# The last layer's MLP output projection as seven block products instead of eight

## The chip, the cores and the metric

The kernel runs on one core of a Trainium2 chip. The metric is the device time in microseconds of one execution. The kernel before has a median of 1990.09 us over three runs (1988.89 to 1991.19).

## What is computed

A decoder trunk of two layers for 512 tokens of width 1024, all in fp32. Each layer mixes tokens in three parallel branches and then runs an MLP; a final RMS norm follows. The part that matters here is the MLP of the second layer and the final norm:

```python
h2 = rms_norm(x, norm2_w[l]) * (1.0 + sc2) + sh2
x = x + g2 * (jnp.square(jax.nn.relu(h2 @ w_up[l])) @ w_down[l])   # 1024 -> 4096 -> 1024
...
return rms_norm(x, final_norm_w)
```

`g2` has one value for each of the 1024 channels.

## The kernel before

Activations are held transposed, with channels on the 128 partitions and the 512 tokens along the free axis (`xt[m]`, eight tiles). Every fp32 matmul is made of three fast ones: both operands are split into a high part H and a low part L, and `mm3` (L199 to L201) issues H·H, L·H and H·L into one PSUM bank. The weights are stationary and the activations move, 512 columns in each matmul.

A planner walks through `Job`s. A Job is two output blocks of 128 channels over eight blocks of 128 inputs; its weights come in two pieces of 128x1024 (four input blocks by 256 channels). `emit_split` fetches a piece by DMA into `raw`, ACT casts it to H (`wH`, L469), DVE subtracts to get L (`wL`, L470), and 24 matmuls use it. A tile framework gives every engine its own order of instructions from that plan, by dependences, priorities and buffers.

The MLP runs in four quarters of 1024 hidden channels. In each, four up Jobs (192 matmuls) end in relu and square on ACT (L1491, L1492) and a split into `uH` and `uL` on ACT and DVE (L192, L193); then four down Jobs (192 matmuls) end in one DVE instruction for each of the eight blocks, x += g2·y (L1504). In the last layer and last quarter, the last two down Jobs go in halves of 256 tokens (192 half-width matmuls in place of 96), so that the end can start on the first half; their weights and results have the names `paH`, `paL`, `po` and `qk`. There the updated x is transposed on PE (`to_tokens`, L1453) to get tokens on partitions, ACT sums squares (L1456), DVE multiplies by the norm's weight (L1458), and `final` scales by 1/rms (L1470 on ACT, L1472 on DVE) and writes out by DMA (L1473).

Of the kernel before, what the change touches and what calls it, by code (L numbers as in the profile page):

```python
# [106 lines left out]
def paired(fin, a, b):  # L107

    a.fin = b.fin = fin
    a.left = b.left = 2  # L110
    ps = a.pieces() + b.pieces()
    for p in ps:
        p.keep = True
    return [Unit(p, c) for c in HALVES for p in ps]

# [35 lines left out]
def tile_trunk(ctx: ExitStack, tc: tile.TileContext, io, out, depth=DEPTH):  # L151
# [15 lines left out]
    def tmp():  # L167
        return tf.tile([P, T], F32, name="tmp", tag="tmp")
# [278 lines left out]

    def emit_split(p):
        j = p.job
        w = sum(n for _, n in j.cols)  # L450
# [23 lines left out]
    def emit_mm(u, ks):  # L474
        p, c = u.p, u.c
        j = p.job
        if j.ps is None:
# [164 lines left out]
    def layer(l, lys):  # L642
# [790 lines left out]

        w_up = io["w_up"][l].rearrange("(k p) c -> p k c", p=P)
        w_dn = io["w_down"][l].rearrange("(k p) c -> p k c", p=P)
        if last:
            xw = [pa.tile([P, 4, P], F32, name="xw", tag="pa") for _ in range(8)]
            sqs = fixed(32).rearrange("p (a b) -> p a b", a=4)
            s4 = fixed(4)
            r4 = fixed(4)  # L1440
            q4 = fixed(4)
            fwb = [pa.tile([P, T], F32, name="fwb", tag="pa") for _ in range(2)]
            for i in range(2):
                sync.dma_start(fwb[i], io["final_norm_w"][i * T:(i + 1) * T].rearrange("(o d) -> o d", o=1).broadcast_to([P, T]))
        else:
            yield Stream(fin, "next", ada(l + 1, "next", [2, 3, 0, 1, 4, 5, 8, 9, 6, 7, 10, 11], pa, "pa", 2.0))
# [13 lines left out]

        def final(c):
            t = slice(c.start // P, c.stop // P)
            s_, r_, q_ = s4[:, t], r4[:, t], q4[:, t]
# [136 lines left out]
```

## Time and profile before

| | us |
|---|---|
| median of three runs (1988.89 to 1991.19) | 1990.09 |
| the profiled execution's own time | 1988.82 |
| its span (the trace) | 1987.1 |
| PE busy | 1949.8 (98%) |
| DVE busy | 1277.8 (64%) |
| ACT busy | 871.6 (44%) |

The MLP of the last layer starts at about 1626 us of the span; its last matmul starts at 1977.06. All tables below are of the same profiled execution. Times in them are microseconds from the start of the span unless marked ns; a PE instruction's printed duration overlaps the next one's, so the spacing of starts tells what a matmul costs.

### The profile page before, as it was taken

The page shows a single profiled execution, that of the slowest core. Times are in us where ns is not written, and L with a number is a line of the kernel's source. Part 1 is how long each engine was busy: PE and PEld are TensorE (multiplying, and loading weights), DVE is VectorE, ACT ScalarE, POOL GpSimd, SP SyncE. Part 2 cuts the span into 40 slices and gives each one's busy share as a digit, 9 for nine tenths or more (in the row PEclk, how much of TensorE's full clock was granted, in tenths as well). Part 3 has the DMA queues.
Part 4 walks back from the last instruction along what each step waited for, and adds up shares of the span by engine and source line. Part 5 has one row for each costly group of instructions (what it writes and reads, how often), then busy time and mean ns, then how long its engine had stood idle before and what let it go on. Part 6 is the DMA issues. An engine that isn't in the chain of part 4 may idle for free.

```text
span 1987.1 us, 26736 instructions
## 1 busy us (share of the span) xinstructions
PE 1949.8 (98%) x9940; PEld 1613.1 (81%) x9940; DVE 1277.8 (64%) x2368; ACT 871.6 (44%) x1562; POOL 94.9 (5%) x135
## 2 busy tenths in 40 slices
PE   7998999999999999999999999999999999999998
PEld 5787777788888988888897787778888898888887
DVE  4799768967846986333578985687575572333334
ACT  4453626733534534142545445384343354233243
POOL 0110210100000000000001101001000000000000
PEclk9999999999999999999999999999999999999999
DMA  9864353552444694333425433425233422333321
GB/s 288 222 168 131 107 153 108 156 188 87 136 127 142 223 371 161 95 103 98 118 86 139 113 103 90 118 70 151 67 104 108 156 95 96 96 96 96 95 96 43
DMA packets 249623, 258.30 MB, mean 130 GB/s; under 512 B 33828, under 2 KB 208212, under 8 KB 249492
## 3 DMA queue, kind: packets, MB, share of 16 engines
q1 hardware_dynamic: 248912, 256.45, 42.3%
q8 instruction: 78, 1.28, 0.3%
q14 instruction: 53, 0.43, 0.1%
q10 hardware_dynamic: 356, 0.14, 0.0%
q0 software_dynamic: 224, 0.00, 0.0%
HBM read 232.81 MB, written 6.42 MB: 120 GB/s over the span
## 4 chain that ended last, share of the span: by engine, by line
PE 89%; DVE 5%; DMA 2%; issue 1%; ACT 1%; POOL 1%; SPq 0%; ACTq 0%; POOLq 0%; DVEq 0%
PE acc L199 25%; PE acc L201 25%; PE acc L200 25%; PE qk L225 2%; PE po L1001 1%; PE tr L992 1%; DVE wL L470 1%; PE po L907 1%; PE tr L894 1%; DVE sc L823 1%; PE qk L1204 1%; DVE m L822 1%; DMA araw<-in_ada_w_dram 1%; PE po L201 1%; PE po L200 1%
## 5 line engine op out<-in xcount | busy, mean ns | idle before, releaser
L199 PE MATMUL acc<-aH,wH 128*128 128x512 f32 x1544 | 613.6, 398 | 10.6 <-DVE paL L193 5.3
L201 PE MATMUL acc<-aH,wL 128*128 128x512 f32 x1544 | 606.7, 393 | 0.9 <-DVE wL L470 0.8
L200 PE MATMUL acc<-aL,wH 128*128 128x512 f32 x1544 | 606.5, 393 | 0.0
L469 ACT CAST wH<-raw 128x1024 fp32r<-128x1024 f32 (+2 forms) x290 | 295.2, 1026 | 289.5 <-PE acc L200 250.5
L470 DVE TENSOR_TENSOR wL<-raw,wH 128x1024 fp32r<-128x1024 f32 (+2 forms) x290 | 343.3, 1199 | 16.0 <-ACT wH L469 8.3
L199 PEld LDWEIGHTS acc<-aH,wH 128*128 128x128 f32 x1544 | 291.4, 189 | 72.8 <-DVE paL L193 6.1
L201 PEld LDWEIGHTS acc<-aH,wL 128*128 128x128 f32 x1544 | 291.0, 188 | 62.5 <-DVE wL L470 2.1
L200 PEld LDWEIGHTS acc<-aL,wH 128*128 128x128 f32 x1544 | 291.6, 189 | 57.6 <-issue 0.7
L199 PE MATMUL acc<-uH,wH 128*128 128x512 f32 x448 | 174.9, 390 | 0.0
L201 PE MATMUL acc<-uH,wL 128*128 128x512 f32 x448 | 174.6, 390 | 0.0
L200 PE MATMUL acc<-uL,wH 128*128 128x512 f32 x448 | 174.3, 389 | 0.0
L193 DVE TENSOR_TENSOR uL<-tmp,uH 128x512 fp32r<-128x512 f32 x64 | 43.9, 691 | 189.2 <-ACT uH L192 189.2
L1491 ACT ACTIVATE tmp<-acc 128x512 f32<-128x512 f32 x60 | 35.3, 592 | 220.0 <-PE acc L201 220.0
L1504 DVE SCALAR_TENSOR_TENSOR x<-acc,slab,x 128x512 f32<-128x512 f32 (+1 forms) x64 | 43.8, 716 | 128.7 <-PE acc L201 128.7
L343 DVE SCALAR_TENSOR_TENSOR aacc<-araw,slab,aacc 128x512 f32<-128x512 f32 x140 | 104.0, 749 | 5.7 <-DMA araw<-in_ada_w_dram 4.1
L200 PEld LDWEIGHTS acc<-uL,wH 128*128 128x128 f32 x448 | 84.1, 188 | 17.4
L201 PEld LDWEIGHTS acc<-uH,wL 128*128 128x128 f32 x448 | 84.1, 188 | 17.4
L199 PEld LDWEIGHTS acc<-uH,wH 128*128 128x128 f32 x448 | 84.1, 188 | 17.1
L882 DVE TENSOR_TENSOR_SCAN tmp<-tmp 128x512 f32<-128x512 f32 (+1 forms) x64 | 52.5, 826 | 21.5 <-ACT tmp L875 21.4
L675 POOL TENSOR_TENSOR tmp<-tmp,slab 128x512 f32<-128x512 f32 (+1 forms) x20 | 31.6, 1581 | 719.5 <-DVE tmp L674 708.6
L1312 DVE SCALAR_TENSOR_TENSOR tmp<-tg,acc 128x512 f32<-128x512 f32 x16 | 11.0, 685 | 67.0 <-PE acc L201 67.0
L822 DVE MAX8 m<-sc 128x8 f32<-128x256 f32 (+2 forms) x96 | 52.8, 552 | 1.2 <-POOL sc L800 0.2
(307 smaller groups left out, 3022.1 us busy)
## 6 DMA issues: line engine op xcount, KB each, us to landing
araw<-in_ada_w_dram SPq DMA_DIRECT2D x192, 256.0 KB, 5.4
raw<-in_w_in_dram SPq DMA_DIRECT2D x96, 512.0 KB, 4.1
raw<-in_w_up_dram SPq DMA_DIRECT2D x64, 512.0 KB, 4.6
raw<-in_w_down_dram SPq DMA_DIRECT2D x64, 512.0 KB, 4.6
raw<-in_w_in_dram SPq DMA_DIRECT2D x56, 256.0 KB, 4.4
acb<-acd SPq DMA_DIRECT2D x32, 256.0 KB, 4.6
raw<-in_w_br_ssd_dram SPq DMA_DIRECT2D x16, 512.0 KB, 4.5
raw<-in_w_out_dram SPq DMA_DIRECT2D x16, 512.0 KB, 4.2
```

The lines of the kernel that those rows point to most:

```text
L193: dve.tensor_sub(L, src, H)
L199: pe.matmul(ps, a[0], b[0], start=start, stop=False)
L200: pe.matmul(ps, a[0], b[1], start=False, stop=False)
L201: pe.matmul(ps, a[1], b[0], start=False, stop=stop)
L225: pe.matmul(ps, q[hh][:, cq], k[n][hh][:, ck], start=n == 0, stop=n == 1)
L343: dve.scalar_tensor_tensor(a, raw, cs[:, k:k + 1], a, op0=ALU.mult, op1=ALU.add)
L469: act.copy(H[:, :w], src)
L470: dve.tensor_sub(L[:, :w], src, H[:, :w])
L822: dve.max(out=m8, in_=sc[tb])
L882: dve.tensor_tensor_scan(out=nv, data0=nv, data1=nv, initial=1.0, op0=ALU.mult, op1=ALU.bypass)
L1491: act.activation(r, ps, AF.Relu)
L1504: dve.scalar_tensor_tensor(xt[m][:, c], ps[:, c], mod[l][:, M_G2 + m:M_G2 + m + 1], xt[m][:, c], op0=ALU.mult, op1=ALU.add)
```

## The change

The first layer keeps its code. In the second, `last_mlp` replaces the four quarters. The up Jobs stay. For the down projection of a quarter, the tokens are cut in two halves of 256, the hidden channels into even and odd blocks of 512, and the output channels into two halves of 512; the product of 2x2 by 2x2 blocks is made of seven block products in Winograd's form of Strassen's identity. Now the activations are stationary (blocks of 128x128 tokens) and the weights move, 512 columns in each matmul, so results have tokens on partitions. A product is 4 hidden blocks x 2 token blocks x 3 = 24 matmuls of 512 columns; a quarter has 168, in the order P1, P6, P2, P7, P5, P4, P3.

- Sums of activations (`us`, four of 128x256 for each pair of hidden blocks) and their splits (`ua`, `ub`, `uc`, `ud`) are made on DVE and ACT after the up Jobs.
- Weights of a quarter are fetched raw into eight tiles `rd`; sums of weights (`tt`, or in place in `rd`) are made by eight DVE instructions of 128x1024, and `split_form` makes 14 pieces of 128x1024, each used by 12 matmuls.
- Each product has two PSUM results (`dn`). In the first quarter ACT copies them into twelve accumulators `yacc` in SBUF, later DVE adds to these (`plus`), 16 additions in a quarter, since P1 goes to two accumulators.
- x is transposed to tokens during the first quarter (32 transposes) and put aside in DRAM (`xtd`), and fetched back (`xtok`) in the last quarter.
- In the last quarter the accumulators are combined (`last_of`), multiplied by g2 (`rowb`), added to x, squared on ACT, scaled and written out. The half-width matmuls are gone.

```diff
+class Prod(Job):
+    def __init__(self, name, form, lhs, banks, evac, need=(), pre=None):
+        super().__init__(name, None, 4, [], [0, 1], None, evac, need=need, dve=0.65, pre=pre, step=2)
+        self.form, self.lhs, self.banks = form, lhs, banks
...
+    def split_form(p):
+        j = p.job
+        src = j.form(p.k0 // 2)
+        H, L = (wp.tile([P, 1024], F32R, name=n, tag=n) for n in ("wH", "wL"))
+        with tc.high_priority():
+            act.copy(H, src)
+            dve.tensor_sub(L, src, H)
+        p.H, p.L = ([X[:, k * T:(k + 1) * T] for k in range(2)] for X in (H, L))
+    def product(u):
+        p = u.p
+        j = p.job
+        if j.ps is None:
+            if j.pre is not None:
+                j.pre()
+            j.ps = j.banks()
+        for i in range(2):
+            for k in range(p.nk):
+                kk = p.k0 + k
+                a = [X[:, i * P:(i + 1) * P] for X in j.lhs(kk)]
+                mm3(j.ps[i], a, (p.H[k], p.L[k]), kk == 0, kk == j.nk - 1)
+            if p.last:
+                with tc.high_priority():
+                    j.evac(i, j.ps[i])
+        p.left -= 1
+        if p.last:
+            j.left -= 1
+            j.fin.add(j.name)
...
+            def to_tokens(tb, i):
+                ps = tr_bank()
+                for m in range(4):
+                    pe.transpose(ps[:, m * P:(m + 1) * P], xt[4 * i + m][:, tb * P:(tb + 1) * P], ident)
+                t = tmp()
+                act.copy(t, ps)
+                sync.dma_start(xtd[:, 2 * tb + i, :], t)
...
+            def plus(key, i, src):
+                if (key, i) not in y:
+                    y[key, i] = tf.tile([P, T], F32, name="yacc", tag="yacc", bufs=12)
+                    act.copy(y[key, i], src)
+                else:
+                    dve.tensor_add(y[key, i], y[key, i], src)
+            def into_x(n, i, tb, d, src=None):
+                o = xf[tb, d] = y[n, i]
+                if src is None:
+                    dve.tensor_mul(o, o, rowb["g", d])
+                    dve.tensor_add(o, o, xtok[tb, d])
+                else:
+                    t = tmp()
+                    dve.tensor_mul(t, src, rowb["g", d])
+                    dve.tensor_add(o, o, t)
...
+            def final(tb, d):
+                t = slice(tb, tb + 1)
+                s_, r_, q_ = s4[:, t], r4[:, t], q4[:, t]
+                dve.tensor_add(s_, sqs[:, tb, 0:1], sqs[:, tb, 1:2])
+                rstd_cols(s_, r_, q_)
+                for i in (1 - d, d):
+                    o = xf[tb, i]
+                    if i == d:
+                        dve.scalar_tensor_tensor(o, o, r_, rowb["f", i], op0=ALU.mult, op1=ALU.mult)
+                    else:
+                        act.activation(o, o, AF.Identity, scale=r_)
+                    sync.dma_start(o2[tb * P:(tb + 1) * P, i * T:(i + 1) * T], o)
+            def early(tb, d):
+                squares(tb, d)
+                dve.tensor_mul(xf[tb, d], xf[tb, d], rowb["f", d])
+            def last_of(n, i, ps):
+                def add_(a, b):
+                    dve.tensor_add(y[a, i], y[a, i], y[b, i])
+                if n == 1:
+                    for tb in (i, 2 + i):
+                        back(tb)
+                elif n == 2:
+                    into_x(2, i, i, 0)
+                    early(i, 0)
+                elif n == 7:
+                    add_(7, 1)
+                    add_(4, 7)
+                    into_x(4, i, 2 + i, 0)
+                elif n == 5:
+                    add_(7, 5)
+                    into_x(7, i, 2 + i, 1)
+                    early(2 + i, 1)
+                    add_(3, 1)
+                    add_(3, 5)
+                    into_x(3, i, i, 1)
+                elif n == 4:
+                    into_x(4, i, 2 + i, 0, ps)
+                    squares(2 + i, 0)
+                    final(2 + i, 0)
+                elif n == 3:
+                    into_x(3, i, i, 1, ps)
+                    squares(i, 1)
...
+                        split(r1[:, 0:V], aH, aL)
+                        split(r2, bH, bL)
+                        dve.tensor_add(S[0], r1[:, V:], r2[:, V:])
+                        dve.tensor_sub(S[1], S[0], r1[:, 0:V])
+                        split(c_, cH, cL)
+                        dve.tensor_sub(S[2], r1[:, 0:V], r1[:, V:])
+                        dve.tensor_sub(S[3], r2[:, 0:V], S[1])
+                        split(d_, dH, dL)
...
+                def sums(h, R=R, F=F):
+                    F[3, h], F[2, h] = (wp.tile([P, 1024], F32, name="tt", tag="tt", bufs=4) for _ in range(2))
+                    dve.tensor_sub(F[3, h], R[1, 1, h], R[0, 1, h])
+                    dve.tensor_add(F[2, h], F[3, h], R[0, 0, h])
+                def t1(h, R=R):
+                    dve.tensor_sub(R[0, 1, h], R[0, 1, h], R[0, 0, h])
+                    return R[0, 1, h]
+                def t4(h, R=R, F=F):
+                    dve.tensor_sub(F[2, h], R[1, 0, h], F[2, h])
+                    return F[2, h]
...
+                prods = [(1, raw_(0, 0), "a11"), (6, f_(2), "s2"), (2, raw_(1, 0), "a12"), (7, f_(3), "s3"),
+                         (5, t1, "s1"), (4, t4, "a22"), (3, raw_(1, 1), "s4")]
+                yield from add([Prod(f"p{n}{qt}", form, lhs(a), banks, evac_of(n), pre=exp_ln_set if end and n == 1 else None)
+                                for n, form, a in prods])
...
-            xw = [pa.tile([P, 4, P], F32, name="xw", tag="pa") for _ in range(8)]
-            sqs = fixed(32).rearrange("p (a b) -> p a b", a=4)
-            s4 = fixed(4)
-            r4 = fixed(4)
-            q4 = fixed(4)
-            fwb = [pa.tile([P, T], F32, name="fwb", tag="pa") for _ in range(2)]
...
+            yield from last_mlp()
+            return
...
-        def to_tokens(m, c):
-            tbs = range(c.start // P, c.stop // P)
-            pt = tr_bank()
-            for tb in tbs:
-                pe.transpose(pt[:, tb * P:(tb + 1) * P], xt[m][:, tb * P:(tb + 1) * P], ident)
-            q = tmp()
-            for tb in tbs:
-                act.activation(q[:, tb * P:(tb + 1) * P], pt[:, tb * P:(tb + 1) * P], AF.Square,
-                               accum_out=sqs[:, tb, m:m + 1])
-                dve.tensor_mul(xw[2 * tb + m // 4][:, m % 4, :], pt[:, tb * P:(tb + 1) * P],
-                               fwb[m // 4][:, m % 4 * P:(m % 4 + 1) * P])
...
-                        if last:
-                            to_tokens(m, c)
-                            if m == NK - 1:
-                                final(c)
```

On DVE, before, in a down projection of the middle of the MLP. `wL` is the low part of a weight piece, and L1504 adds a result to x:

```order
L470 TENSOR_TENSOR wL<-raw,wH 128x1024 x2
L1504 SCALAR_TENSOR_TENSOR x<-acc,slab,x 128x512 x2
L470 TENSOR_TENSOR wL<-raw,wH 128x1024 x2
L1504 SCALAR_TENSOR_TENSOR x<-acc,slab,x 128x512 x2
L470 TENSOR_TENSOR wL<-raw,wH 128x1024 x2
```

On DVE, after, in the products of the third quarter (L463 makes a piece's low part, L1531 adds a result to its accumulator, L1639, L1640 and L1647 are sums of weights):

```order
L463 TENSOR_TENSOR wL<-rd,wH 128x1024
L1639 TENSOR_TENSOR tt<-rd 128x1024
L463 TENSOR_TENSOR wL<-tt,wH 128x1024
L1531 TENSOR_TENSOR yacc<-yacc,dn 128x512
L1640 TENSOR_TENSOR tt<-tt,rd 128x1024
L1531 TENSOR_TENSOR yacc<-yacc,dn 128x512
L463 TENSOR_TENSOR wL<-tt,wH 128x1024
L1639 TENSOR_TENSOR tt<-rd 128x1024
L463 TENSOR_TENSOR wL<-rd,wH 128x1024
```

Between two splits there stand now a sum of weights and additions to accumulators, where two x additions stood between pairs of splits.

On DVE, before, at the end of the last quarter, up to the first half's output:

```order
L1504 SCALAR_TENSOR_TENSOR x<-po,slab,x 128x256
L1504 SCALAR_TENSOR_TENSOR x<-qk,slab,x 128x256
L1458 TENSOR_TENSOR xw<-tr,fwb 128x128 x4
L1464 TENSOR_REDUCE slab<-slab 128x2
L362 TENSOR_SCALAR slab<-slab 128x2
```

On DVE, after, in the middle of the last quarter's products (L1563, L1568, L1537 and L1538 are steps of the output on accumulators; `udL` is the low part of the last pair's S3 and S4):

```order
L1563 TENSOR_TENSOR yacc<-yacc,rowb 128x512 x2
L1568 TENSOR_TENSOR yacc<-yacc 128x512 x2
L463 TENSOR_TENSOR wL<-tt,wH 128x1024
L1531 TENSOR_TENSOR yacc<-yacc,dn 128x512 x2
L1568 TENSOR_TENSOR yacc<-yacc 128x512 x2
L1537 TENSOR_TENSOR yacc<-yacc,rowb 128x512 x2
L1538 TENSOR_TENSOR yacc<-yacc,xtok 128x512 x2
L202 TENSOR_TENSOR udL<-us,udH 128x512
L1647 TENSOR_TENSOR tt<-rd,tt 128x1024
L1531 TENSOR_TENSOR yacc<-yacc,dn 128x512 x2
```

The output's steps stand among the pieces' splits instead of behind the last result, and eight of them stand ahead of `udL` and of the sum L1647 that the next products take.

On PE, after, the place that takes this `udL` (the matmuls on `ubH` and `ubL` are of another product):

```order
L208 MATMUL dn<-wH,ubH 128x512
L209 MATMUL dn<-wL,ubH 128x512
L210 MATMUL dn<-wH,ubL 128x512
L210 MATMUL dn<-wH,udL 128x512 x2
L208 MATMUL dn<-wH,ubH 128x512 x2
L208 MATMUL dn<-wH,udH 128x512 x2
L209 MATMUL dn<-wL,ubH 128x512
```

The last two matmuls of P7 stand behind work of P4, which the order took ahead of them.

Elsewhere in the program rows move by a few places (PE at some 50 rows, some DMA issues of the first layer's weights), and buffers lie at other addresses.

## Rows read from the trace of the kernel before

**Rows 1.** Page, parts 1 and 4: busy time of each engine; the last chain by engine.
```profile
PE 1949.8 (98%) x9940; PEld 1613.1 (81%) x9940; DVE 1277.8 (64%) x2368; ACT 871.6 (44%) x1562; POOL 94.9 (5%) x135
...
PE 89%; DVE 5%; DMA 2%; issue 1%; ACT 1%; POOL 1%; SPq 0%; ACTq 0%; POOLq 0%; DVEq 0%
```

**Rows 2.** Windows of the last layer's MLP; the columns stand in the first line.
```profile
core 0: us, PE busy (x) PEld busy (x) DVE busy (x) ACT busy (x) POOL busy (x), PEclk, DMA share, GB/s
1717.00:1804.00 87.00, 87.00 (x386) 72.03 (x385) 29.42 (x32) 28.88 (x40) 0.00 (x0) 1.00 0.31 97
1804.00:1891.00 87.00, 87.00 (x386) 72.03 (x385) 29.41 (x32) 28.88 (x40) 0.00 (x0) 1.00 0.31 97
1891.00:1977.00 86.00, 86.00 (x484) 75.34 (x483) 34.39 (x70) 37.03 (x101) 0.00 (x0) 1.00 0.18 61
1977.00:1988.00 11.00, 1.17 (x7) 0.54 (x6) 3.81 (x14) 3.18 (x12) 0.00 (x0) 0.72 0.26 95
```

**Rows 3.** Groups by line, 1629 to 1988 us: names, shapes, count | busy, mean ns | idle before.
```profile
L470 DVE TENSOR_TENSOR wL<-raw,wH 128x1024 fp32r<-128x1024 f32 x54 | 63.6, 1217 | 0.0
...
L193 DVE TENSOR_TENSOR uL<-tmp,uH 128x512 fp32r<-128x512 f32 x32 | 22.0, 692 | 120.5 <-ACT uH L192 120.5
...
L1504 DVE SCALAR_TENSOR_TENSOR x<-acc,slab,x 128x512 f32<-128x512 f32 x28 | 20.1, 750 | 86.2 <-PE acc L201 86.2
...
L1453 PE MATMUL tr<-slab,x 128*128 128x128 f32 x32 | 5.7, 282 | 0.2 <-DVE x L1504 0.2
```

**Rows 4.** PE in order of time, down projection: start, us, line, operation.
```profile
1720.27 0.39 PE L199 MATMUL acc<-aH,wH 128*128 128x512 f32 x1
1720.50 0.39 PE L200 MATMUL acc<-aL,wH 128*128 128x512 f32 x1
1720.72 0.39 PE L201 MATMUL acc<-aH,wL 128*128 128x512 f32 x1
1720.95 0.39 PE L199 MATMUL acc<-aH,wH 128*128 128x512 f32 x1
```

**Rows 5.** Chain of waits near the end: start, us, engine, tile, line (half-width matmuls).
```profile
1974.11 0.12 PE qk L199
1974.22 0.12 PE qk L200
1974.35 0.12 PE qk L201
```

**Rows 6.** DVE in order of time, back to back: start, us, line, operation.
```profile
641.55 0.42 DVE L410 TENSOR_TENSOR tmp<-tmp 128x256 f32<-128x256 f32 x1
641.89 0.69 DVE L470 TENSOR_TENSOR paL<-raw,paH 128x512 fp32r<-128x512 f32 x1
642.49 0.42 DVE L410 TENSOR_TENSOR tmp<-tmp 128x256 f32<-128x256 f32 x1
...
667.29 4.85 DVE L343 SCALAR_TENSOR_TENSOR aacc<-araw,slab,aacc 128x512 f32<-128x512 f32 x7
...
1078.97 1.19 DVE L470 TENSOR_TENSOR wL<-raw,wH 128x1024 fp32r<-128x1024 f32 x1
1080.10 0.73 DVE L798 SCALAR_TENSOR_TENSOR sc<-tmp,slab,sc 128x512 f32<-128x512 f32 x1
```

**Rows 7.** All engines in order of time, the last ten microseconds.
```profile
1977.06 0.28 PE L201 MATMUL qk<-uH,paL 128*128 128x256 f32 x1
...
1980.63 0.16 DVE L365 TENSOR_TENSOR slab<-slab 128x2 f32<-128x2 f32 x1 [0.51 <-ACT slab L364]
1980.82 0.16 DVE L366 TENSOR_TENSOR slab<-slab 128x2 f32<-128x2 f32 x1
...
1981.42 1.33 ACT L1470 ACTIVATE xw<-xw,slab 128x512 f32<-128x512 f32 x2 [0.82 <-DVE slab L368]
1981.42 0.88 DVE L1472 TENSOR_SCALAR xw<-xw,slab 128x512 f32<-128x512 f32 x2
1981.93 1.79 SPq L1473 DMA_DIRECT2D out_dram<-xw  x4
```

**Rows 8.** Page, part 6: DMA issues, count, size of each, median us to landing.
```profile
raw<-in_w_down_dram SPq DMA_DIRECT2D x64, 512.0 KB, 4.6
```

**Rows 9.** Windows of other stages, columns as in rows 2.
```profile
150.00:200.00 50.00, 44.66 (x201) 35.47 (x200) 49.28 (x109) 17.90 (x29) 1.50 (x5) 0.93 0.44 129
```

More of the change, by code (lines that the diff above doesn't have):

```diff
@@ L446, in add @@
                                      op0=ALU.add, op1=ALU.subtract)
+    def split_form(p):
[25 more added lines that the diff above has]
+            j.fin.add(j.name)
     def emit_split(p):
         j = p.job
+        if isinstance(j, Prod):
+            split_form(p)
+            return
         w = sum(n for _, n in j.cols)
@@ L476, in emit_mm @@
         j = p.job
+        if isinstance(j, Prod):
+            product(u)
+            return
         if j.ps is None:
@@ L1436, in layer @@
         if last:
-            xw = [pa.tile([P, 4, P], F32, name="xw", tag="pa") for _ in range(8)]
-            sqs = fixed(32).rearrange("p (a b) -> p a b", a=4)
-            s4 = fixed(4)
-            r4 = fixed(4)
-            q4 = fixed(4)
-            fwb = [pa.tile([P, T], F32, name="fwb", tag="pa") for _ in range(2)]
[L1443 to L1446, printed above, removed]
@@ L1461, in final @@
-        def final(c):
-            t = slice(c.start // P, c.stop // P)
-            s_, r_, q_ = s4[:, t], r4[:, t], q4[:, t]
-            dve.tensor_reduce(out=s_, in_=sqs[:, t, :], op=ALU.add, axis=mybir.AxisListType.X)
-            rstd_cols(s_, r_, q_)
-            for tb in range(t.start, t.stop):
-                for i in range(2):
-                    o = xw[2 * tb + i]
-                    if i:
-                        act.activation(o, o, AF.Identity, scale=r4[:, tb:tb + 1])
-                    else:
-                        dve.tensor_scalar(o, o, r4[:, tb:tb + 1], None, op0=ALU.mult)
-                    sync.dma_start(o2[tb * P:(tb + 1) * P, i * T:(i + 1) * T], o.rearrange("p m c -> p (m c)"))
+            yield from last_mlp()
@@ L1475, in dn_pre @@
+            return
+        yield Stream(fin, "next", ada(l + 1, "next", [2, 3, 0, 1, 4, 5, 8, 9, 6, 7, 10, 11], pa, "pa", 2.0))
+        ss = SumSq()
         def dn_pre():
             exp_ln_set()
-            if not last:
-                lys[l + 1] = begin(l + 1)
-                scale_of(l + 1, lys[l + 1]["A1"], M_SC1, "norm1_w")
+            lys[l + 1] = begin(l + 1)
+            scale_of(l + 1, lys[l + 1]["A1"], M_SC1, "norm1_w")
         for qt in range(4):
@@ L1506, in evac_dn @@
                     if qt == 3:
-                        if last:
-                            to_tokens(m, c)
-                            if m == NK - 1:
-                                final(c)
-                        else:
-                            ss.add(xt[m], c, m)
-                            if m == NK - 1:
-                                norm1(l + 1, lys[l + 1], ss, c)
+                        ss.add(xt[m], c, m)
+                        if m == NK - 1:
+                            norm1(l + 1, lys[l + 1], ss, c)
                 end = qt == 3 and mp == 3
@@ L1519, in layer @@
                                  evac_dn, kbase=8 * qt, dve=1.3, each=qt == 3 and mp >= 2,
-                                 need=["next"] if end and not last else ["ada.11"], pre=dn_pre if end else None))
+                                 need=["next"] if end else ["ada.11"], pre=dn_pre if end else None))
             yield from add(downs[:2])
```

105 lines of the change are left out of this document (added).

## The prediction

> **What bounds the kernel now.** I read the page's busy shares and the chain first. PE is busy 98% of the span and carries 89% of the chain that ended last; DVE has 64% [rows 1]. A share is an average over stages, so the windows of the last layer's MLP come next: in three of them PE is busy 87.00 of 87.00 us (or 86.00 of 86.00) at a granted clock of 1.00, DVE 29.4 to 34.4 us [rows 2]. The only wait of PE for another engine there is 0.2 us, ahead of the transposes [rows 3]. So the stage is as long as its matmuls: four start within 0.68 us, 0.2267 us each [rows 4], and half-width ones at 0.12 us [rows 5]. Each matmul taken out there is time gained, as long as DVE, idle for two thirds of the stage, can feed PE. Last I read the end: the last matmul starts at 1977.06 and the span ends at 1987.1, ten microseconds in which PE does next to nothing [rows 2, 7].
>
> **What the change removes on PE.** Before, a quarter's down projection has 192 full-width matmuls, after it 168. In three quarters that is 3 x 24 x 0.2267 = 16.3 us. In the last quarter 96 full and 192 half-width ones (21.8 + 23.0 = 44.8 us) give way to 168 x 0.2267 = 38.1 us: 6.7 us. Together **23.0 us**. The 32 transposes stay (they move from the end to the first quarter), one small one is added: 0.1 us. Without any wait PE would end at 1977.3 - 22.9 = 1954.4, and the last product phase, 38.1 us long, would begin at T = 1916.3.
>
> **What it adds on DVE in a product phase.** I take DVE's price of an instruction by the spacing of starts when several follow each other, not by the printed duration: 1.13 us for 1024 columns (1078.97 to 1080.10; printed 1.19, mean 1.217), 0.60 us for 512 (641.89 to 642.49; printed 0.69), 0.34 us for 256 (641.55 to 641.89; printed 0.42) [rows 3, 6]. A phase of the second and third quarter holds 14 splits of weight pieces and 8 sums of weights (22 x 1.13 = 24.9 us), 16 additions to accumulators (9.6 us), and what is left of the last up pair: five instructions of 256 columns and three of 512 (3.5 us). That is 38.0 us beside PE's 38.1 us, and 40.3 with the two splits which the next up Jobs want before the phase ends. Before, a whole window of 87 us had 29.4 us of DVE work [rows 2]. **DVE becomes level with PE in these phases**, where it had been idle most of the time. A piece now feeds 12 matmuls, 2.72 us, where it fed 24, 5.44 us; with two buffers of `wL` DVE can run hardly more than a piece ahead. Walking the order row by row with these prices, PE waits a little for the eighth, tenth, eleventh and thirteenth piece: 0.3, 0.2, 0.6 and 0.3 us, some 1.4 us in each of the two phases. The bounds: 0, if the additions slip behind the splits, and 4.3 us, if every DVE instruction took its full duration (42.4 us of work). In the first quarter ACT makes 12 of the 16 additions as copies, so DVE has 24 x 1.13 + 4 x 0.60 + 3.5 = 33 us: I take 0.5 us of waiting (0 to 1). Sum: **3.3 us**, so T = 1919.6.
>
> The weights' transfers are no larger: 4 MB in a quarter as before, 4.6 us from issue to landing of each 512 KB [rows 8], and issued ahead in eight buffers. Putting x aside in DRAM and fetching it adds 2 MB in gaps where the DMA share is 0.18 to 0.31 [rows 2], and its consumers come in the last quarter: nothing. ACT has 14 casts where it had 16; nothing.
>
> **The last quarter and the end.** Here the output's arithmetic comes on top, on 512-column rows of tokens. From T + 2.7 us, when the first product is under way, the order puts on DVE: 12 splits and 2 sums of weights (14 x 1.13 = 15.8 us), 53 instructions of 512 columns (31.8), five of 256 (1.7), 20 to 24 on one column (0.2 each by the spacing of the norm's small steps [rows 7]; 4.8) and four scalings of 512 with a scalar (0.66 each, the spacing of such instructions [rows 6]; 2.7). That is 56.8 us, against 38.1 us of PE. So **DVE sets the end of this phase, not PE.** `udL` stands behind eight output steps, and PE waits for it with work of the next products queued behind, for some 2.7 us; then for the last sum of weights' split (1.8) and others (1.0). PE ends at about T + 43.7, while DVE is busy until T + 59.5; I add 1.0 us for the places where DVE in turn waits for PE's late results: T + 60.5 = 1980.1. From the last arithmetic to the span's end the kernel before needs 4.3 us (two scalings on DVE begin at 1981.42, on ACT the pair takes 1.33 us and ends at 1982.75; the span ends at 1987.1) [rows 7]; I take the same, as the same 256 KB tiles are written. End: 1984.4, that is **2.7 us earlier** than 1987.1. Of the 23 us, 3.3 go to the phases before, and about 17 to DVE's list behind the last matmul and PE's waits for it. The profiled execution's own time is 1988.82, so 1986.1 beside it; against the median, 1990.09 - 2.7 = 1987.4.
>
> The price of a DVE instruction decides this, and the printed rows speak for the shorter one: the next instruction starts 0.06 to 0.09 us before the one in front of it ends [rows 6]. The Trainium skill ("VectorE: DVE Perf Modes", "The DRAIN you can't avoid") says the contrary, that the next operation doesn't start until the pipe is empty. By that rule each instruction would cost its full duration; the rows here don't agree with it for instructions that are ready, and it is one reason why the first rival has a chance at all.
>
> **Rivals.**
> *Slower: DVE pays the full duration.* The rows of rows 6 are of instructions that were ready. In the product phases most instructions are held by a cast on ACT, a result on PE, or the instruction in front (chains of multiply and add on one accumulator). If such a one starts only after the one before has ended, the prices are 1.22, 0.69 and 0.75 us [rows 3]: the waits ahead of T are 1 + 4.3 + 4.3 = 9.6 us (T = 1925.9), the last phase's list 14 x 1.22 + 53 x 0.69 + 2.1 + 4.8 + 3.0 = 63.6 us, the end T + 2.7 + 63.6 + 1 + 4.3 = 1997.5: 10.4 us later, 2000.5 against the median. Break-even lies a fifth of the way from spacing to duration: 1.15 us for 1024 columns and 0.62 for 512. For it: the order alternates pieces, sums and additions, with a wait at almost each. Against it: such a wait costs only if its releaser is late, and DVE with a backlog finds them done.
> *Faster: no waits ahead of T, no idle DVE behind it.* If the additions slip without delaying a split, T = 1916.3, and the end is 1916.3 + 2.7 + 56.8 + 4.3 = 1980.1: 7 us earlier, 1983.1. For it: two phases in which DVE and PE are level are preceded by up phases in which DVE has room. Against it: a piece is needed each 2.72 us, and two sums and two additions in a row take longer.
> *The clock falls.* Where PE had waits between other work, the granted clock was 0.93 (busy 44.66 of 50 us) [rows 9]. In the last quarter PE would have about 38 of 44 us; 7% of 38 is 2.7 us, but DVE sets the end there, so it costs up to that only where PE's result holds DVE: within the range.
> *The change does not do what it says elsewhere.* The other rows that move are few and in stages that PE fills: within 1 us either way.
>
> **How the numbers follow.** My forecast, 1987.4 with its own spread of some 4 us, has 0.43; the faster rival 0.28; the slower one 0.26; the rest something not seen, mostly slower. The range reaches from the faster rival less 1.5 us, for DVE and PE both better than walked, to the slower one: 1981.5 to 2000.5. Within 0.2% (4 us, about what a measurement of this kernel can tell from no change) is 1986.1 to 1994.1: the forecast lies near its lower edge, so a part of its own chance falls to faster, and part of the slower rival, half reached, stays within. Faster 0.38, same 0.36, slower 0.26.
>
> **What would show it.** In the profile after: PE's matmuls in the stage fall by 16.3 + 6.7 us at unchanged spacing; DVE near 100% busy in the last 60 us; PE waiting for `udL` and `wL` some 5 us in the last quarter, about 1.4 us in the second and third; some 20 us from the last matmul to the end instead of 10. If starts on DVE lie 1.2 and 0.69 us apart in the product phases, the slower rival is right. If DVE has gaps in the last 60 us, or PE waits for something else (a transfer of `rd`, a PSUM bank), my list is not what bounds it.

## The result, and the profile after

The changed kernel has a median of 2000.86 us (six runs, 1999.68 to 2007.41) beside 1988.72 for the kernel before in six runs of the same session (1987.16 to 1991.19). The ratio is 1.0065, with a 95% interval of 1.005 to 1.008: **slower by 0.65%**, some 12 to 13 us. The prediction was 1987.4, in a range of 1981.5 to 2000.5, with most of its chance on faster (0.38) or no change (0.36).

The profiled execution spans 2000.2 us, against 1987.1. Parts 1 and 4 of the page after (busy time of three engines; the last chain by engine and by line) answer to [rows 1]:

```profile
PE 1937.6 (97%) x9749; PEld 1593.5 (80%) x9749; DVE 1407.1 (70%) x2546; ACT 924.7 (46%) x1605; POOL 93.8 (5%) x135
...
PE 78%; DVE 10%; DMA 6%; ACT 2%; issue 2%; POOL 0%; SPq 0%; DVEq 0%; ACTq 0%; POOLq 0%
```

PE has 12.2 us less to do, and its share of the chain falls from 89% to 78%, while DMA's rises from 2% to 6%. Six per cent of 2000 us is 120 us of chain on transfers, in a change that was not meant to touch a transfer outside the last layer's MLP. That is the first hint that the loss is not where the code was changed.

The second step is to put the same PE instruction of both traces side by side and note how late the changed kernel is. The names and the order are the same nearly everywhere ahead of the last MLP, so this can be done from the first microsecond on:

| start before, us | 607 | 667 | 788 | 1029 | 1149 | 1602 | 1624.50 |
|---|---|---|---|---|---|---|---|
| after is later by | 2.0 | 5.4 | 9.5 | 11.9 | 12.8 | 13.1 | 18.9 |

The last column is the second pair of the norm's matmuls, right ahead of the last MLP. The 2.0 us up to 607 are within what executions differ by at that point (of the runs below, e6_early is there 3.4 us early and e1_room 0.9 us late). PE in order of time, before:

```profile
1624.50 0.70 PE L420 MATMUL qk<-tmp,slab 128*128 128x256 f32 x2
```

and after:

```profile
1643.44 0.59 PE L429 MATMUL qk<-tmp,slab 128*128 128x256 f32 x2
```

From there to the end the kernel before takes 1987.1 - 1624.5 = 362.6 us and the changed one 2000.2 - 1643.4 = 356.8. **The MLP that was changed gained 5.8 us; 18.9 us were lost ahead of it**, in code that is the same word for word.

The windows of the last MLP after (from the first product of each quarter to that of the next, then the last quarter's products, then the end) answer to [rows 2]:

```profile
core 0: us, PE busy (x) PEld busy (x) DVE busy (x) ACT busy (x) POOL busy (x), PEclk, DMA share, GB/s
1689.50:1771.10 81.60, 81.60 (x361) 67.57 (x360) 52.53 (x66) 44.88 (x67) 0.00 (x0) 1.00 0.34 104
1771.10:1852.90 81.80, 81.80 (x361) 67.42 (x360) 59.57 (x78) 39.00 (x55) 0.00 (x0) 1.00 0.34 103
1852.90:1934.90 82.00, 82.00 (x363) 67.35 (x361) 60.70 (x79) 40.52 (x59) 0.00 (x0) 1.00 0.27 84
1934.90:1980.50 45.60, 41.62 (x170) 32.80 (x168) 40.99 (x58) 17.53 (x29) 0.00 (x0) 0.93 0.17 58
1980.50:2000.50 20.00, 0.20 (x1) 0.00 (x0) 14.06 (x43) 7.99 (x24) 0.00 (x0) 0.62 0.28 105
```

A quarter takes 82 us where it took 87, PE is full in three of them, and the end has the 20 us without PE that the prediction spoke of.

**Where the 18.9 us went.** The waits for transfers between 620 and 800 us (engine, tile, line, whom it waited for: us in total, times, longest) before, while layer 0's MLP runs, the weights of the modulation, `araw`, are streamed beside it, and DVE sums them up in `aacc`:

```profile
ACT aacc L341 <- DMA araw<-in_ada_w_dram: 20.1, 4, 7.2
```

and after (622 to 810 us; the last row is a wait of PE's own):

```profile
DVE aacc L352 <- DMA araw<-in_ada_w_dram: 20.8, 23, 3.1
ACT aacc L350 <- DMA araw<-in_ada_w_dram: 19.3, 7, 8.1
...
ACT wH L510 <- DMA raw<-in_w_up_dram: 8.1, 4, 3.4
...
PE acc L210 <- DVE wL L511: 2.3, 5, 0.6
```

DVE did not wait for `araw` before; now it waits 23 times, and ACT waits for `raw`, the pieces of PE's own weights. What holds the transfers is seen on the queue of SP, which issues them in order. Its wait for the sums in `aacc` between 600 and 800 us, before:

```profile
SPq L339 <- DVE aacc L343: 2.9, 7, 1.4
```

and after:

```profile
SPq L348 <- DVE aacc L352: 34.8, 38, 7.1
```

SP waits for DVE to have finished with an `araw` tile before it can load the next one into the same place, and the loads of `raw` stand behind it in the queue. The addresses in the compiled program tell why. The 96 tiles of `araw` that are streamed here lie at 42 different addresses before and at 31 after; but after, 47 of the 96 take turns at only three of these, where the three most used ones had 14. (The first 64 tiles of the stream, which DVE sums up before 520 us, lie at 18 addresses before and at 3 after. At 607 us the changed kernel is late by only 2.0 us, so that is not where the time went.) The loads of `raw` lie at 6 addresses before, each with 32 to 71 of 318; after, 268 of 286 lie at three. Of the 318 tiles of `wL`, 289 lie at two addresses after, where five had 49 to 74 each. The framework lays out the on-chip memory for the whole program at once. It first looks for a layout in which a tile is placed, where possible, at an address that some time has passed for since its last use, and where that search gives up, it makes one without that preference, everywhere. Of the kernels here, the changed one and e2_held8 (below) have this second layout. In the changed kernel the tiles of the new MLP (`rd`, `tt`, `yacc`, `rowb`, `xtok` and those of the sums) made the search for the first fail.

The chain of waits at the end of the second layer's mixing stage, after (start, us, engine or transfer, tile, line), shows what the second layout does to a load:

```profile
1597.23 3.48 DMA raw<-in_w_out_dram
1600.73 0.63 ACT paH L510
1601.42 0.57 issue
1602.00 1.23 DVE wL L511
1603.24 5.14 DMA raw<-in_w_out_dram
...
1614.04 4.66 DMA raw<-in_w_up_dram
1618.72 1.05 ACT wH L510
1619.80 1.23 DVE wL L511
1621.06 3.91 DMA raw<-in_w_up_dram
1624.99 1.05 ACT wH L510
1626.07 1.23 DVE wL L511
```

Load, cast, subtraction, and only then the next load: they take turns. Before, the same stretch of the chain holds nothing but matmuls. PE runs dry at 1623: it is busy 2.36 of the 5 us to 1628, and in the next 5 us the granted clock is 0.75. These two places, 607 to 788 us and the 22 us ahead of the last MLP, account for 7.5 and 5.8 of the 18.9 us; what makes the 3.6 us between them is open.

```profile
1623.00:1628.00 5.00, 2.36 (x20) 2.16 (x18) 1.93 (x3) 1.33 (x2) 0.00 (x0) 1.00 0.86 290
1628.00:1633.00 5.00, 3.82 (x21) 3.77 (x22) 2.84 (x7) 4.09 (x9) 0.00 (x0) 0.75 0.01 1
```

### The profile page after: what moved, and what is told of

Same layout as the page of the kernel before. It is cut to its first block, busy times and chain, and to the rows that moved or that the text cites. A ratio compares the mean times of both kernels' runs of the same rounds, so it can differ in the third digit from the quotient of the medians.

```text
span 2000.2 us, 26789 instructions
## 1 busy us (share of the span) xinstructions
PE 1937.6 (97%) x9749; PEld 1593.5 (80%) x9749; DVE 1407.1 (70%) x2546; ACT 924.7 (46%) x1605; POOL 93.8 (5%) x135
## 4 chain that ended last, share of the span: by engine, by line
PE 78%; DVE 10%; DMA 6%; ACT 2%; issue 2%; POOL 0%; SPq 0%; DVEq 0%; ACTq 0%; POOLq 0%
PE acc L208 20%; PE acc L209 20%; PE acc L210 20%; DMA araw<-in_ada_w_dram 3%; PE qk L234 2%; PE dn L208 2%; PE dn L209 2%; PE dn L210 2%; DVE wL L511 2%; DMA raw<-in_w_up_dram 1%; DVE sc L867 1%; DVE aacc L352 1%; PE po L1045 1%; DVE tmp L926 1%; DVE m L866 1%
## 5 line engine op out<-in xcount | busy, mean ns | idle before, releaser
L210 PE MATMUL acc<-uH,wL 128*128 128x512 f32 x224 | 87.4, 390 | 0.5 <-DVE wL L511 0.5
L208 PE MATMUL acc<-uH,wH 128*128 128x512 f32 x224 | 87.8, 392 | 0.0
L209 PE MATMUL acc<-uL,wH 128*128 128x512 f32 x224 | 87.2, 389 | 0.0
L867 DVE MATCH_REPLACE8 sc<-m,sc 128x256 f32<-128x256 f32 (+2 forms) x96 | 51.9, 541 | 0.0
L208 PE MATMUL acc<-paH,wH 128*128 128x512 f32 x128 | 49.9, 390 | 0.0
L210 PEld LDWEIGHTS acc<-uH,wL 128*128 128x128 f32 x224 | 42.0, 188 | 9.7 <-DVE wL L511 0.9
L210 PE MATMUL acc<-paH,wL 128*128 128x512 f32 x128 | 49.8, 389 | 0.0
L209 PE MATMUL acc<-paL,wH 128*128 128x512 f32 x128 | 49.8, 389 | 0.0
L209 PEld LDWEIGHTS acc<-uL,wH 128*128 128x128 f32 x224 | 42.1, 188 | 8.6
L208 PEld LDWEIGHTS acc<-uH,wH 128*128 128x128 f32 x224 | 42.1, 188 | 8.5
```

What stands on the lines that cost most here:

```text
L208: pe.matmul(ps, a[0], b[0], start=start, stop=False)
L209: pe.matmul(ps, a[0], b[1], start=False, stop=False)
L210: pe.matmul(ps, a[1], b[0], start=False, stop=stop)
L867: dve.match_replace(out=sc[tb], in_to_replace=m8, in_values=sc[tb], imm_value=TAKEN)
```

## The experiments

**1 and 2. The layout without the change, and the change with the other layout.** Theory A: the layout costs what is lost ahead of the last MLP. Theory B: the new code itself does it, by its instructions or transfers.

*e2_held8* is the kernel before with tiles that are held through the last MLP and do nothing:

```diff
+        def hold(src):
+            for n in range(8):
+                held.append(wp.tile([P, 1024], F32, name="hold", tag="hold", bufs=8))
+                act.copy(held[n][:, 0:1], src[:, 0:1])
```

> The kernel before, with eight tiles of 128x1024 held idle in SBUF through the last MLP (32 KB of each partition; each written in one column by ACT after the first up result and again in the last quarter: 16 small copies). Nothing else is added. The layout of the whole program then moves as in the changed kernel: the same 20 rows on PE, 22 on DVE and 27 DMA issues move, the weight stream's tiles lie on 3 addresses instead of 18, raw on 3 instead of 6. Theory A: the loss comes without any product being changed: the norm's pair ahead of the last MLP at 1635 to 1645 us instead of 1624.5, total 10 to 20 us above the kernel before: 1999 to 2009. Rival B: idle tiles cost nothing but 16 copies on an idle ACT: 1988 to 1991.

Measured: 2012.05 us, ratio 1.0108 (1.0091 to 1.0124), by 3 us more than the 1999 to 2009 that theory A expected. *e2_held6* has six such tiles in place of eight:

> The control of the run with eight held tiles: the same with six (24 KB, 12 small copies). Here every engine's order stays that of the kernel before, and so do the addresses (18 for the weight stream, 6 for raw). Theory A: as the kernel before, 1988 to 1990. A rival by which the small copies or the held bytes themselves cost something: three quarters of what eight cost.

Measured: 1991.74 us, ratio 1.0009 (0.9997 to 1.0021). With six, the tiles of `raw` lie where the kernel before has them, and those 96 of `araw` at 42 addresses as there; with eight, as in the changed kernel, 47 of the 96 tiles of `araw` share three addresses, and all loads of `raw` do. Two idle tiles more, and 20 us are gone. The waits of e2_held8 between 620 and 805 us and of its SP queue between 600 and 800 us are those of the changed kernel:

```profile
DVE aacc L343 <- DMA araw<-in_ada_w_dram: 19.9, 21, 3.1
```

```profile
SPq L339 <- DVE aacc L343: 36.2, 37, 7.1
```

Beside the kernel before it is late by 3.4 us at 667, 9.0 at 788, 12.3 at 1029, 13.2 at 1602 and 18.7 at the norm's pair, as the changed kernel is (5.4, 9.5, 11.9, 13.1 and 18.9), and from the pair to the end it takes 2005.8 - 1643.2 = 362.6 us, exactly what the kernel before takes. So the layout, with the few rows that move with it, makes the loss without a line of the change. How large the loss is, one profile tells only to some 5 us: in e2_held6, whose order is that of the kernel before and whose addresses hardly differ from it, the pair starts at 1629.6 and not at 1624.5, since the stretch from 1029 to 1400 us takes 4.9 us more in that execution.

*e1_room* goes the other way: the changed kernel with fewer bytes, so that the first layout fits. The sums of weights are made in place, and the raw weights lie in one large tile:

```diff
-                    F[3, h], F[2, h] = (wp.tile([P, 1024], F32, name="tt", tag="tt", bufs=4) for _ in range(2))
-                    dve.tensor_sub(F[3, h], R[1, 1, h], R[0, 1, h])
-                    dve.tensor_add(F[2, h], F[3, h], R[0, 0, h])
+                    dve.tensor_sub(R[1, 1, h], R[1, 1, h], R[0, 1, h])
...
-                    R[e, d, h] = wp.tile([P, 1024], F32, name="rd", tag="rd", bufs=8)
+                    R[e, d, h] = ar["rd"][:, k * 1024:(k + 1) * 1024]
```

> The changed kernel with less SBUF in its last MLP: the eight raw weight tiles are slices of one tile, the sums of weights are made in place (no tt tiles; the two raw pieces that P3 takes are fetched a second time, 1 MB more in a quarter), and the rows for the output come later. With that, every engine's order ahead of the last MLP is again that of the kernel before, and tiles there have the kernel before's spread of addresses (the weight stream's tiles of layer 0 on 18 addresses instead of 3, raw on 6 instead of 5). Theory A (the loss comes ahead of the last MLP, from tiles placed on addresses that were released just before, so that loads wait): the norm's second matmul pair ahead of the last MLP starts at 1624.5 us as in the kernel before (1643.4 in the changed one), and the total is that of the kernel before less the 5.8 us that the MLP gains from there to the end: 1983 us, 1980 to 1986. Rival B (the loss is in the seven products themselves, in DVE or in transfers of weights, and the late start is something that every form of the change has): 1998 to 2003, the pair at about 1643.

Measured: 1988.0 us, ratio 0.9985 (0.9975 to 0.9995). Some 13 us are back, which B didn't allow; but 5 us are missing from the 1983 that A expected, and the pair starts at 1632.1, not at 1624.5. Some 4 of these lie ahead of the MLP again, and are of another kind. Layer 0's down projection in e1_room, PE in order of time:

```profile
805.40 0.40 PE L208 MATMUL acc<-uH,wH 128*128 128x512 f32 x1
805.63 0.39 PE L209 MATMUL acc<-uL,wH 128*128 128x512 f32 x1
805.86 0.40 PE L210 MATMUL acc<-uH,wL 128*128 128x512 f32 x1
806.10 0.39 PE L208 MATMUL acc<-uH,wH 128*128 128x512 f32 x1
```

The starts are 0.2333 us apart and not 0.2267 as in [rows 4]; the mean over the stage's 672 matmuls is 0.2341 against 0.2277 in the kernel before, which makes 4.3 us. Nothing waits there. What differs is the address of the moving operands: `uH` and `uL` lie 12,864 bytes lower in a partition than in the kernel before and the changed one.

**3. The same room with smaller tiles.** *e3_room4* cuts the large tile into four, which puts `uH` and `uL` back where they were:

```diff
-                        ar["rd"] = wp.tile([P, 8 * 1024], F32, name="rda", tag="rda", bufs=1)
+                        ar[k // 2] = wp.tile([P, 2048], F32, name="rda", tag="rda", bufs=4)
```

> As the run with more room (raw weights in one tile of 32 KB), but with that tile cut in four of 8 KB. In that run the large tile pushed uH and uL, the moving operands of layer 0's down projection, to other addresses (16512 instead of 29376 in each partition), and there its trace has their matmuls 0.2333 us apart instead of 0.2267, 768 of them: 5 us, while the MLP at the end, from the norm's matmuls on, was 8 us shorter than in the kernel before. Here uH and uL lie at 29376 again, and every engine's order ahead of the last MLP is still that of the kernel before. If the spacing comes with the place of the operand: 0.2267 again, and the whole gain of the last MLP shows: 1980 us where the kernel before has 1988.7, ratio 0.995 to 0.997. If it was a whim of that execution or chip, or comes with something else in this form: as that run, ratio 0.998 to 0.999.

Measured: 1984.63 us, ratio 0.9974 (0.9963 to 0.9985), faster than the kernel before and than e1_room, but a little short of the 0.995 to 0.997 that was expected. The matmuls of layer 0 are 0.2277 us apart on the mean again:

```profile
805.34 0.39 PE L209 MATMUL acc<-uL,wH 128*128 128x512 f32 x1
805.57 0.39 PE L210 MATMUL acc<-uH,wL 128*128 128x512 f32 x1
805.79 0.39 PE L208 MATMUL acc<-uH,wH 128*128 128x512 f32 x1
```

So the change, in this form, is worth 0.26% once it doesn't spoil the layout of the rest. From the norm's pair to the end this kernel takes 1983.4 - 1628.7 = 354.7 us, 2.1 less than the changed one and 7.9 less than the kernel before, of which the medians show 4.4. In this profile 6.4 us are lost between 1029 and 1400 us, the stretch that differed in e2_held6 too.

**4. Is it DVE's list that sets the end?** The prediction's main step for the last quarter. Two runs take work off DVE and give it to POOL; two move it to an earlier phase. *e4_pool* is e3_room4 with 16 of the output's steps on POOL:

```diff
+                if src is None and n != 3:
+                    pool.tensor_tensor(out=o, in0=o, in1=rowb["g", d], op=ALU.mult)
+                    pool.tensor_tensor(out=o, in0=o, in1=xtok[tb, d], op=ALU.add)
...
+                pool.tensor_tensor(out=xf[tb, d], in0=xf[tb, d], in1=rowb["f", d], op=ALU.mult)
```

> The kernel with four tiles of raw weights, and 16 of the last quarter's output steps (multiply by g2, add x, multiply by the norm's weight on accumulators of P2, P4 and P7) on POOL instead of DVE. If DVE's list sets the end, as the forecast had it, DVE has 16 x 0.60 = 9.6 us less behind the first product, and the end comes 5 to 9 us earlier than with the four tiles alone (some of it is lost again where the order puts a sum of weights behind additions that wait for PE): 1971 to 1975 us where the kernel before has 1988.7. If POOL's steps (1.6 us each where the kernel before has one such) become the end, or POOL slows DVE down: no gain, 1979 to 1985.

Measured: 1993.01 us, ratio 1.0021 (1.0009 to 1.0033): slower than e3_room4 by 8 us, where 5 to 9 less were expected, or no gain. PE's longest wait from 1640 us on (first row), and ACT's wait for POOL from 1630 on (second):

```profile
PE dn L208 <- ACT wH L462: 14.9, 1, 14.9
```

```profile
ACT tmp L1550 <- POOL yacc L1540: 27.5, 3, 20.1
```

ACT's sum of squares waits for POOL's slow step, and the cast of the next weight piece stands behind it on ACT. That alone would be a matter of order, so *e5_pool_first* gives the sums of weights a high priority, ahead of the output's steps:

```diff
-        src = j.form(p.k0 // 2)
+        with tc.high_priority():
+            src = j.form(p.k0 // 2)
```

> As the run with output steps on POOL, and the sums of weights get the same high priority as the splits that use them, so that they stand ahead of output steps and additions in DVE's order. If waits of PE in the last quarter (2.4 us for udL, 1.6 us and more for splits in the changed kernel) come from what stands ahead of these on DVE: PE's waits in the last quarter fall under 2 us, and the end comes 2 to 4 us earlier than without: 1968 to 1972 us where the kernel before has 1988.7. If the waits only move to the outputs behind: no difference to the run without.

Measured: 1994.37 us, ratio 1.0027 (1.0017 to 1.0036), the same as without. The long wait is gone, and the time is not: from the last quarter's first product to the end it takes 70.8 us where e4_pool takes 73.0, but from the norm's pair to that product 294.8 where e4_pool takes 291.2. DVE in order of time while POOL works:

```profile
1934.00 1.22 DVE L1661 TENSOR_TENSOR rda<-rda 128x1024 f32<-128x1024 f32 x1
...
1943.85 2.29 DVE L464 TENSOR_TENSOR wL<-rda,wH 128x1024 fp32r<-128x1024 f32 x1
1946.06 1.75 DVE L202 TENSOR_TENSOR udL<-us,udH 128x512 fp32r<-128x512 f32 x1
...
1967.99 0.68 DVE L1547 TENSOR_TENSOR tmp<-dn,rowb 128x512 f32<-128x512 f32 x1
```

and POOL:

```profile
1941.77 1.60 POOL L1541 TENSOR_TENSOR yacc<-yacc,xtok 128x512 f32<-128x512 f32 x1
1943.34 3.92 POOL L1569 TENSOR_TENSOR yacc<-yacc,rowb 128x512 f32<-128x512 f32 x2
...
1965.28 3.93 POOL L1541 TENSOR_TENSOR yacc<-yacc,xtok 128x512 f32<-128x512 f32 x2
```

While POOL has a step of 128x512 under way, a DVE instruction with two operands in SBUF takes 2.29 us in place of 1.22, or 1.75 in place of 0.69: 1.06 to 1.07 us more at either width. One with an operand in PSUM (`dn`) keeps its 0.68. The Trainium skill ("SBUF — State Buffer", "Who interferes with whom") says that a DVE instruction with two SBUF inputs contends with a GpSimd instruction that reads SBUF, since its second input comes through a shared read interface, and one with at most one SBUF input, outside the modes that use both ports, does not; these rows agree on both. DVE lost more time than POOL took over: with 16 instructions fewer, it is busy 60.7 us (e4_pool) and 60.5 us (e5_pool_first) from 2.7 us behind the last quarter's first product to its last instruction, where e3_room4 has 54.5. So these two runs did not shorten DVE's list, and don't test the step that they were made for.

*e6_early* keeps everything on DVE and shortens the list: during the last up phase, where DVE has room, the accumulators are combined, multiplied by g2, and x is added, so that a product is added to a running sum:

```diff
+            def combine():
+                for i in range(2):
+                    for a, b in ((7, 1), (4, 7), (3, 1), (3, 5), (7, 5)):
+                        dve.tensor_add(y[a, i], y[a, i], y[b, i])
...
+                elif n == 2:
+                    dve.tensor_add(w, w, ps)
+                    scaled(2, w, w)
+                    early(i, 0)
```

> The kernel e3_room4 with the output's arithmetic of the last quarter cut: while its up phase runs, the accumulators of the first three quarters are added together (10 instructions on VectorE), multiplied by the output factors, and x is added (16 instructions); in the product phase a product is then added once to a running sum instead of to several accumulators, so VectorE has 38 instructions of 512 columns there instead of 53. TensorE's work is the same. Theory A (VectorE's list sets the end of the last quarter, as the prediction has it): 15 instructions at their measured spacing of 0.60 us are 9.0 us; some 1 to 2 us of it are lost where VectorE then waits for TensorE's products, so the span ends 7 to 9 us earlier than that of e3_room4: time 1976 to 1978, against the kernel before 0.993 to 0.994, and the last VectorE instruction about 52 us behind the quarter's first product instead of about 60. Theory B (TensorE's waits for weight pieces, not VectorE's list, set the end): TensorE ends where it did, and the time stays at 1983 to 1986.

Measured: 1975.46 us, ratio 0.992 (0.9905 to 0.9936). In its profile the last quarter's products start at T = 1915.20. The last matmul:

```profile
1953.05 0.39 PE L210 MATMUL dn<-wH,udL 128*128 128x512 f32 x1
```

and the last of DVE:

```profile
1965.84 0.75 DVE L1564 SCALAR_TENSOR_TENSOR yacc<-yacc,slab,rowb 128x512 f32<-128x512 f32 x1
```

PE's last matmul starts at T + 37.9, which is 167 x 0.2267 without a wait (e3_room4: T + 44.3), DVE ends at T + 51.4 (T + 57.8), and the span at T + 56.1 (T + 63.2): 7.1 us less. The traces have 53 instructions of 512 columns on DVE behind T + 2.7 in e3_room4 (the four scalings at the end not counted) and 41 in e6_early. That is 12 fewer, not the 15 that the expectation counted, and 12 x 0.60 = 7.2 us.

PE ends 6.4 us earlier too, so the two ends alone don't tell which engine set the time. DVE's busy time from T + 2.7 to its last instruction does, in e3_room4 and in e6_early (columns as in the windows above):

```profile
1922.95:1978.06 55.11, 38.10 (x157) 29.72 (x155) 54.53 (x100) 22.70 (x49) 0.00 (x0) 0.88 0.26 92
1917.90:1966.59 48.69, 35.54 (x157) 29.09 (x155) 47.47 (x88) 23.94 (x48) 0.00 (x0) 0.89 0.15 54
```

DVE has no more than 0.6 and 1.2 us of idle time there, and its list is shorter by 7.1 us. And in e1_room PE's last matmul starts at T + 45.5, 1.2 us later than in e3_room4, while DVE ends at T + 57.8 in both.

The medians of the two kernels, from different sessions, lie 9.2 us apart (the kernel before was 2.1 us slower in the session of e6_early), and the two profiled spans 12.1. Of these 4.6 lie ahead of the norm's pair, most of it between 1080 and 1400 us, in the stretch whose length differs by several microseconds from one execution to another.

*e7_early_first* puts the sums of weights first in addition, by the edit of e5_pool_first:

> The kernel e6_early with the sums of weights put ahead of everything else that VectorE could do, so that the pieces udL and wL are made earlier. Theory A: with VectorE's list shorter than in e3_room4, TensorE's waits for udL and wL (some 3.5 us in the last quarter there) shrink by 1 to 3 us, output arithmetic moves behind them, and the time is that of e6_early or up to 2 us less: 1974 to 1978. If the sums now delay the output arithmetic as much as they help TensorE, the time is that of e6_early within 1 us. Theory B: TensorE's waits set the end, so the time falls by what the waits fall, from 1984 to 1981 or so.

Measured: 1979.08 us, ratio 0.9943 (0.9926 to 0.9959): slower than e6_early, where no loss over 1 us was expected. From T to the end it takes 56.4 us, the same; but from the norm's pair to T it takes 294.4 us where e6_early takes 291.1. With its waits for `udL` already gone, PE had nothing to gain in the last quarter, and in the first three the sums pushed ahead cost 3.3 us. In the profile PE's own wait for `wL` there is 2.0 us; the rest isn't traced to its cause.

## Why the prediction was wrong

*The step that failed* is the last of the rivals: "The other rows that move are few and in stages that PE fills: within 1 us either way." It measured +18.9 us in the profile, and e2_held8 shows nearly the same (+18.7) without the change. The rows that moved (20 on PE, 22 on DVE, 27 on SP ahead of the last MLP) came with another layout of the whole program. The waits that grew are those of loads for the last use of their address; what the moved rows cost by themselves no run separates. That buffers lie at other addresses was seen and written down ahead of the prediction, and it was put at nothing. What it would have had to price is in the rows above: a load of a weight piece takes 3.5 to 5.1 us, its cast 1.05 and its subtraction 1.23, and they lie beside matmuls only as long as there is a free address for the next load.

*The rest, in its order.*

- PE's saving of 23.0 us: right in what was taken out. A quarter is 5.44 us shorter (24 x 0.2267), less waits.
- Waits in the first three quarters, 0.5, 1.4 and 1.4 us: measured 0, 0.22 and 0.34, by how the lead on the kernel before grows from quarter to quarter (5.44, 5.22, 5.10). This is the faster rival's case ahead of T, in which additions slip without delaying a split. DVE has 60 us of work in 82 where it had 29 in 87 [rows 2], and still feeds PE.
- T, the start of the last products: 1919.6 predicted. Measured 1934.88, less 18.94 ahead of the MLP: 1915.9. Too late by 3.7 us, 2.7 of them by the waits.
- The list on DVE: T + 60.5 predicted for its end, T + 59.9 measured (1994.82), and from T + 2.7 on it was busy 54.7 of 57.2 us. So the list was 2.1 us shorter than the 56.8 predicted, and DVE stood still for 2.5 us instead of 1.0: that the end fits to 0.6 us is in part luck. The price by spacing, 1.13 and 0.60 us, was right, so *the slower rival is false though its time, 2000.5, came out*, by luck, from a loss elsewhere. DVE in the last products:

```profile
1949.76 1.22 DVE L463 TENSOR_TENSOR wL<-tt,wH 128x1024 fp32r<-128x1024 f32 x1
1950.89 1.50 DVE L1531 TENSOR_TENSOR yacc<-yacc,dn 128x512 f32<-128x512 f32 x2
1952.32 1.22 DVE L463 TENSOR_TENSOR wL<-tt,wH 128x1024 fp32r<-128x1024 f32 x1
1953.45 1.29 DVE L1537 TENSOR_TENSOR yacc<-yacc,rowb 128x512 f32<-128x512 f32 x2
1954.66 1.22 DVE L463 TENSOR_TENSOR wL<-rd,wH 128x1024 fp32r<-128x1024 f32 x1
```

The starts lie 1.13 us behind an instruction of 1024 columns and 1.21 behind two of 512 (1.43 in the first pair), although each split needs a cast from ACT. The rule that the prediction quoted from the Trainium skill ("VectorE: DVE Perf Modes", "The DRAIN you can't avoid") would make them 1.22 and 1.38; the rows don't agree with it. The same section adds that a next operation that is not held starts earlier, which the prediction left out, and with that these rows agree.

- PE in the last quarter: its waits, some 5 us, were 4.0, for the operands named and one cast:

```profile
PE dn L210 <- DVE udL L202: 2.4, 1, 2.4
PE dn L208 <- ACT wH L462: 1.6, 1, 1.6
```

- Its last matmul starts at T + 45.4, not at T + 43.7, since behind those two waits the granted clock fell to 0.50 from 1970 to 1975 us (the lower level, 1.2 GHz), with matmuls 0.43 us apart. This was the rival of the clock. It reached the end only where DVE waited for PE: DVE is busy 3.60 of those 5 us, and its one gap of more than 0.25 us behind T + 2.7, 1.97 us, lies there.
- From the list's end to the span's end 4.3 us were taken, 5.4 measured. The end is at T + 65.3 where T + 64.8 was predicted.
- In the last quarter PE waited for no transfer of `rd` and for no PSUM bank.
- Two small slips in the sums: the bound of 4.3 us for full durations comes out at some 4.0 by the prices given, and the seven merged instructions of [rows 6] are 0.68 us apart, not 0.66. Neither moves the forecast by more than 0.1 us.

In sum the MLP by itself was predicted at -2.7 us and gave -5.8, for T. The step that DVE's list sets the end was right: e6_early has 12 instructions fewer on it and ends 7 us earlier.

## What to carry to other kernels

Where a framework lays out on-chip memory for the whole program, a change in one stage can cost time in every other: compare how many loads of each streamed tile share an address, and where that rises, price the loads as taking turns with their use. The number of different addresses alone misleads: here it fell from 42 to 31 for the stream that waited, and from 18 to 3 for the one that cost 2 us at most. Compare the traces instruction by instruction from the start before looking at the changed stage; a loss that is there before the first changed instruction runs is not the change's own work. And a change that frees PE pays only as far as the next engine's list is cut with it: with the layout kept and the output's additions moved to a phase where DVE has room, the same seven products gave 0.8% instead of a loss.

## What the runs showed that was not expected

- POOL's 128x512 steps on tiles in SBUF lengthen a concurrent DVE instruction with two SBUF operands by 1.06 to 1.07 us, and take 1.3 to 2.3 us themselves (e4_pool, e5_pool_first). Here DVE was busy 6 us longer for giving 16 instructions away.
- The moving operands' place went with a spacing of matmuls of 0.2333 instead of 0.2267 us at the full granted clock, with nothing waiting: 4.3 us over 672 matmuls (e1_room against e3_room4). Only those two layouts were compared, and other tiles moved as well, so the address as the cause is likely and not shown; nor is what about an address would do it.
- Two waits of PE of 2.4 and 1.6 us within 5 us were followed by some 5 us at half the granted clock, while DVE and ACT went on (busy 3.60 and 1.37 of those 5 us).
